# Making the high halves of the mixer's weights on GpSimd instead of ScalarE, in a two-layer encoder

## The chip, the core and the metric

The kernel runs on one core of a Trainium2 chip. The core has five engines with their own instruction queues: TensorE (PE in the profile; its weight loads are shown apart as PEld), VectorE (DVE), ScalarE (ACT), GpSimd (POOL) and SyncE (SP, which here only issues DMAs). Each queue runs in order, and an instruction waits on semaphores for what other engines or DMAs must have done. The metric is the device time of one execution in microseconds (us), less being better. Before the change it is 616.48 us, the median of three runs (616.14 to 616.51).

## What is computed

Two encoder layers over 256 tokens of width 1024. Each layer has a mixer and a feed-forward part, all in float32:

```python
def mixer_sublayer(x, ...):
    h = rms_norm(x, n1)
    proj = h @ w_in_l                       # 1024 -> 2560
    qa, ka, va, qd, kd, vd, qc, kc, vc = jnp.split(proj, cuts, axis=-1)
    ...                                     # q and k: rms_norm per head, rotary for d and c
    out_a = neighbourhood_attention(...)    # 4 heads
    out_d = dilated_window_attention(...)   # 6 heads
    out_c = gqa_block_attention(...)        # 6 query heads, 2 key/value heads
    mix = jnp.concatenate([rms_norm(out_a, ...), rms_norm(out_d, ...), rms_norm(out_c, ...)], axis=-1)
    return x + mix @ w_out_l                # 1024 -> 1024

def channel_sublayer(x, n2, w_gu, cw, cb, w_dn):
    h = rms_norm(x, n2)
    g, u = jnp.split(h @ w_gu, 2, axis=-1)  # 1024 -> 2 x 2816
    g = depthwise_conv_centred(g, cw, cb)
    return x + (jax.nn.gelu(g, approximate=False) * u) @ w_dn
```

## The kernel before, in words

**Split products.** TensorE multiplies fp32r numbers, so each float32 operand is written as a high part (the number copied into the type fp32r) and a low part (the number less its high part, again fp32r). A product then takes three matmuls: high by high, high by low, low by high (`mm3`, line 636). The weights arrive as float32 and are split on the core.

**Weight units.** All weights are cut into units of at most 2048 numbers per partition, in the order in which TensorE needs them (`units_of`, line 544). A layer has 18 units for its mixer and 33 for its feed-forward. The mixer's are, by the names in `PROJ_NAMES`: two each for dq, dk, dv, cq (8 units, 1536 wide), one for ckv, two for aqk, one for av (4 units, 2048 wide), and six for the output projection (four 1536 and two 1024 wide). `PER_LAYER` is 51 and `LAST_OUT` is 18, so `i % PER_LAYER < LAST_OUT` holds for unit `i` if it belongs to a mixer.

**What happens to a unit.** `load(i)` (line 581) has SP fetch it into one of four buffers `raw`. `split(i)` (line 607) makes the high part in one of two buffers `hi` and the low part in one of two buffers `lo`, in chunks: 384 wide for the 1536-wide projection units, 512 wide for most others, and 1024 for the feed-forward's down units. For each chunk ScalarE copies `raw` into `hi`, and VectorE subtracts: `lo = raw - hi`. Both inputs of that subtraction lie in SBUF. A `hi` buffer comes free when TensorE has finished the unit two before, a `raw` buffer when VectorE has made the last low chunk from it; then SP can fetch the unit four later. The six output-projection units of the second layer are an exception: `keep` (line 565) splits them during the first layer's feed-forward, puts both parts into DRAM, and GpSimd's DMA queue fetches them back, so `split` has nothing to do for them.

**Other work in the mixer.** The queries and keys are normalised per head (`normed`, line 901): ScalarE squares, VectorE or ScalarE sums, GpSimd computes `rstd` by two small instructions (a scale-and-add called `ms`, and a power called `rstd`), and VectorE or ScalarE scales. `rotated` (line 931) is five or more VectorE instructions on SBUF operands (`sw`, `z`). GpSimd also builds the rotary tables (`cd`, `sd`, `cc`, `sc`), spreads the neighbourhood bias with one copy of 28 partitions by 1984 (`na_repeat`, line 756), adds squares (`sqm`) and computes the group `rstd` that the output projections wait for (`group_rstd`, line 1073). Softmax and the transposed probabilities go over ScalarE and VectorE.

**Order.** The program does not emit instructions directly. `Plan` records every operation with its dependencies; `order()` (line 303) then goes through them with a table of costs (`cost`, line 416) and of hand-over times between engines, and always emits the operation that its own clock says can start first, the earlier in the program on a tie. So every instruction is issued from one line (413), and a changed cost or engine for one operation may change the order of all others, on all engines.

Of the kernel before, what the change touches and what calls it, by code (L numbers as in the profile page):

```python
# [37 lines left out]
BANK = 512  # L38
# [183 lines left out]
class Plan:  # L222
# [30 lines left out]
    def add(self, engine, method, args, kw):  # L253
# [14 lines left out]
        if method == "matmul" and not kw["start"]:  # L268
            ins.append(args[0])
        o.ns, o.size = cost(engine.name, method, args, kw, ins)  # L270
        o.before, o.after, o.first, o.tiles = set(), [], [], []
        for v in ins + outs:
# [143 lines left out]
def cost(engine, method, args, kw, ins):  # L416

    out = args[0]
    if method == "dma_start":
        w = out if isinstance(out, View) else args[1]  # L420
        small = min(out.shape[-1], args[1].shape[-1]) < 128
        return 460, 4 * math.prod(w.shape) * (2 if small else 1)
    n = out.width()
    psum = any(v.tile.pool.psum for v in ins)
    if engine == "PE":
        if method == "transpose":
            return 110, 0
        n = args[2].width()
        if args[1].dtype == F32:
            return 108, 0  # L430
        if args[1].shape[0] < P:
            return n / 4.8 + 15, 0
        return n / (2.4 if args[1].dtype == F32R else 1.2) + 2.5, 0
    if engine == "ACT":
        extra = 93 * sum(isinstance(kw.get(k), View) for k in ("scale", "bias")) + 90 * ("accum_out" in kw)
        return 0.833 * n + (47 if psum else 94) + extra, 0
    if engine == "DVE":
        if method in ("reduce_sum", "reduce_max"):
            n = args[1].width()
        per = 1.04  # L440
        if method in ("tensor_copy", "tensor_scalar_mul") and not psum:
            per = 0.52
        if method == "tensor_tensor_reduce":
            per = 1.3
        return per * n + (130 if method == "scalar_tensor_tensor" or method == "tensor_scalar_mul" and n > 16 else 70), 0
    if method == "memset":
        return 40 + 0.9 * n, 0
    if method == "tensor_copy":
        return 3.4 * n, 0
    if kw.get("op") == ALU.pow:  # L450
        return 300 + 165 * n, 0
    return 2.2 * n + 160, 0
# [3 lines left out]
def encoder_kernel(  # L456
# [21 lines left out]
    nc = Plan(tc)  # L478
# [82 lines left out]
    PER_LAYER = len(views) // DEPTH  # L561
    LAST_OUT = PER_LAYER - len(FFN)
# [44 lines left out]
    def split(i):  # L607
        v = views[i]
        a, b = v.shape[1], v.shape[2]
        n = a * b  # L610
        raw = raws[i]
        hi = wp.tile([P, UNIT], F32R, tag="hi", name=f"hi{i}", bufs=PARTS)
        lo = wp.tile([P, UNIT], F32R, tag="lo", name=f"lo{i}", bufs=PARTS)
        h = b if i < 2 else b * max(1, CHUNK // b)
        if i in kept:
            for d, z in zip(kept[i], (hi, lo)):
                nc.gpsimd.dma_start(z[:, :n], d)
        for c in range(0, n if i not in kept else 0, h):
            e = min(c + h, n)
            nc.scalar.copy(hi[:, c:e], raw[:, c:e])  # L620
            nc.vector.tensor_tensor(lo[:, c:e], raw[:, c:e], hi[:, c:e].bitcast(F32), op=ALU.subtract)
        r = lambda z: z[:, :n].rearrange("p (a b) -> p a b", b=b)
        parts.append((r(hi), r(lo)))

    def unit():

        i = taken[0]
        taken[0] += 1
        with nc.later(SPLIT_LATER):
            while len(raws) < min(i + AHEAD + RAWS - PARTS, len(views)):  # L630
                load(len(raws))
            while len(parts) < min(i + AHEAD, len(views)):
                split(len(parts))
        return parts[i]
# [181 lines left out]
    for l in range(DEPTH):  # L816
# [3 lines left out]
        if l == 0:  # L820
            gains_T(0, 1)
            split(0)
# [624 lines left out]
```

## Time and profile before

| | us |
|---|---|
| median of three runs | 616.48 |
| the profiled execution, whole | 616.62 |
| its span in the trace | 614.9 |
| PE busy | 605.8 |
| DVE busy | 487.4 |
| ACT busy | 428.1 |
| POOL busy | 82.5 |

The whole time of the profiled execution is 1.7 us more than its span. The granted TensorE clock was 0.999. Times inside the trace are given in us from the start of the span. The first layer's mixer takes about the first 128 us, its feed-forward runs to about 312, the second layer's mixer to about 426, the second feed-forward to the end. Busy times are unions per engine; a matmul's end is modelled, so PE's busy share says that PE was never long without an instruction, not that it ran at its peak. In the chain of waits, a stretch that is "PE" from piece to piece is one in which TensorE was held up by nothing but itself.

### The profile page before, as it was taken

How to read it: one execution, taken by the hardware profiler on the slowest of the kernel's cores; microseconds unless marked ns; L12 is line 12 of the kernel's file. 1: busy time of each engine (PE TensorE's matmuls, PEld its weight loads, DVE VectorE, ACT ScalarE, POOL GpSimd, SP SyncE). 2: the span in 40 equal slices, each digit the busy share in tenths (PEclk: the TensorE clock that was granted, in tenths of full speed). 3: DMA queues.
4: the chain of work that ended last, by engine and by line, in shares of the span. 5: the costliest groups of instructions: out<-in, count | busy, mean ns of one | idle time of the engine just before them, and what ended most of it. 6: DMA issues, size and time to landing. Idle time of an engine off the chain costs nothing.

```text
span 614.9 us, 9864 instructions
## 1 busy us (share of the span) xinstructions
PE 605.8 (99%) x3484; PEld 523.8 (85%) x3484; DVE 487.4 (79%) x1000; ACT 428.1 (70%) x1064; POOL 82.5 (13%) x136
## 2 busy tenths in 40 slices
PE   8999999999999999999999999999999999999997
PEld 6998878888888888888899988887888888888885
DVE  4898989897777988887867797867977777777774
ACT  6788989686566676666588898866755656556651
POOL 2731230211400000000022212332000000000000
PEclk9999999999999999999999999999999999999999
DMA  8794312655596999978444744553565556555501
GB/s 279 273 290 156 102 36 86 227 191 194 169 244 237 366 350 325 312 272 277 154 151 153 243 136 173 201 179 119 200 228 174 173 202 203 173 176 202 187 20 68
DMA packets 85073, 121.44 MB, mean 198 GB/s; under 512 B 9864, under 2 KB 69608, under 8 KB 85024
## 3 DMA queue, kind: packets, MB, share of 16 engines
q1 hardware_dynamic: 82752, 112.17, 55.3%
q0 software_dynamic: 1728, 8.39, 3.8%
q8 instruction: 27, 0.44, 0.3%
q10 hardware_dynamic: 544, 0.26, 0.2%
q14 instruction: 22, 0.18, 0.1%
HBM read 110.93 MB, written 9.88 MB: 196 GB/s over the span
## 4 chain that ended last, share of the span: by engine, by line
PE 93%; DVE 2%; ACT 2%; issue 1%; DMA 1%; POOL 0%; SPq 0%; DVEq 0%; ACTq 0%
PE psw_w L413 50%; PE psa_a L413 43%; DVE const_x L413 1%; ACT act_s2k L413 1%; DMA wp_raw<-in_w_in_dram 1%; DVE act_hT L413 1%; ACT act_hT L413 1%; ACT wp_hi L413 0%; DVE wp_lo L413 0%; POOL small_rstd L413 0%; ACT act_mixT_hi L413 0%; POOL small_ms L413 0%; SPq L413 0%; DVE act_mixT_lo L413 0%; DVE small_ss L413 0%
## 5 line engine op out<-in xcount | busy, mean ns | idle before, releaser
L413 DVE TENSOR_TENSOR wp_lo<-wp_raw,wp_hi 128x512 fp32r<-128x512 f32 (+2 forms) x332 | 232.9, 732 | 43.8 <-ACT wp_hi L413 42.3
L413 PE MATMUL psw_w<-act_hT,wp_hi 128*128 128x512 f32 x704 | 248.6, 397 | 0.4 <-DVE act_hT L413 0.4
L413 ACT CAST wp_hi<-wp_raw 128x512 fp32r<-128x512 f32 (+2 forms) x332 | 203.2, 661 | 27.0 <-PE psw_w L413 15.5
L413 PE MATMUL psw_w<-act_hT,wp_lo 128*128 128x256 f32 x704 | 196.5, 280 | 0.0
L413 PEld LDWEIGHTS psw_w<-act_hT,wp_hi 128*128 128x128 f32 x704 | 132.0, 188 | 32.6 <-DVE act_hT L413 1.1
L413 PEld LDWEIGHTS psw_w<-act_hT,wp_lo 128*128 128x128 f32 x704 | 132.7, 189 | 1.1
L413 PE MATMUL psa_a<-wp_hi,act_hT 128*128 128x384 f32 (+2 forms) x448 | 112.8, 332 | 0.7 <-ACT act_hT L413 0.5
L413 ACT COPY act_s2k<-psw_w 128x256 f32<-128x256 f32 x88 | 32.3, 372 | 74.5 <-PE psw_w L413 74.5
L413 PEld LDWEIGHTS psa_a<-wp_hi,act_hT 128*128 128x128 f32 x448 | 77.9, 189 | 3.8 <-ACT act_hT L413 1.0
L413 PE MATMUL psa_a<-wp_lo,act_hT 128*128 128x384 f32 (+2 forms) x224 | 74.8, 335 | 0.0
L413 PE MATMUL psa_a<-wp_lo,act_ch 128*128 128x512 f32 x176 | 69.5, 395 | 0.0
L413 PE MATMUL psa_a<-wp_hi,act_ch 128*128 128x512 f32 x176 | 69.4, 394 | 0.0
L413 PE MATMUL psa_a<-wp_hi,act_cl 128*128 128x512 f32 x176 | 65.8, 394 | 0.0
L413 DVE TENSOR_TENSOR act_s2k<-psw_w,act_s2k 128x256 f32<-128x256 f32 x88 | 36.8, 422 | 30.1 <-ACT act_s2k L413 29.7
L413 PEld LDWEIGHTS psa_a<-wp_lo,act_hT 128*128 128x128 f32 x224 | 42.3, 189 | 2.3 <-DVE wp_lo L413 1.3
L413 PEld LDWEIGHTS psa_a<-wp_hi,act_cl 128*128 128x128 f32 x176 | 33.2, 188 | 7.8
L413 PEld LDWEIGHTS psa_a<-wp_hi,act_ch 128*128 128x128 f32 x176 | 33.1, 188 | 7.8
L413 PEld LDWEIGHTS psa_a<-wp_lo,act_ch 128*128 128x128 f32 x176 | 33.1, 188 | 6.9
L413 DVE SCALAR_TENSOR_TENSOR act_s2k<-act_s2k,act_cw,act_s2k 128x255 f32<-128x255 f32 x88 | 36.9, 478 | 1.5 <-ACT act_s2k L413 1.3
L413 POOL TENSOR_TENSOR small_rstd<-small_ms,const_mh 128x6 f32<-128x6 f32 (+2 forms) x26 | 31.4, 1208 | 2.2
L413 ACT ACTIVATE act_s2k<-act_s2k,act_cw 128x256 f32<-128x256 f32 x44 | 24.1, 595 | 10.0 <-DVE act_s2k L413 9.6
L413 PE MATMUL psw_w<-act_ch,const_v 128*128 128x256 f32 x128 | 28.6, 286 | 1.1 <-ACT act_s2k L413 1.1
(112 smaller groups left out, 779.1 us busy)
## 6 DMA issues: line engine op xcount, KB each, us to landing
wp_raw<-in_w_gate_up_dram SPq DMA_DIRECT2D x44, 1024.0 KB, 5.1
wp_raw<-in_w_down_dram SPq DMA_DIRECT2D x22, 1024.0 KB, 4.8
wp_raw<-in_w_in_dram SPq DMA_DIRECT2D x14, 768.0 KB, 5.5
wp_raw<-in_w_in_dram SPq DMA_DIRECT2D x8, 1024.0 KB, 5.6
wp_raw<-in_w_out_dram SPq DMA_DIRECT2D x8, 768.0 KB, 6.3
dram_khi<-act_mixT_hi SPq DMA_DIRECT2D x4, 768.0 KB, 4.4
dram_klo<-act_mixT_lo SPq DMA_DIRECT2D x4, 768.0 KB, 5.8
wp_lo<-dram_klo POOLq DMA_DIRECT2D x4, 768.0 KB, 4.8
```

The source lines that it names most:

```text
L413: getattr(o.engine.real, o.method)(*map(real, o.args), **{k: real(v) for k, v in o.kw.items()})
```

## The change

In `split`, the high part of each chunk of a mixer unit is made by `gpsimd.tensor_copy` in place of `scalar.copy`, from the third unit of the program on. The first two units, all feed-forward units, and the units that `keep` handles stay with ScalarE. The planner's cost of a GpSimd copy of up to 512 elements becomes 0.92 n + 150 ns; wider ones (the bias copy) keep 3.4 n.

```diff
@@ cost
     if method == "tensor_copy":
-        return 3.4 * n, 0
+        return (3.4 * n if n > BANK else 0.92 * n + 150), 0
@@ split
         for c in range(0, n if i not in kept else 0, h):
             e = min(c + h, n)
-            nc.scalar.copy(hi[:, c:e], raw[:, c:e])
+            if i >= 2 and i % PER_LAYER < LAST_OUT:
+                nc.gpsimd.tensor_copy(hi[:, c:e], raw[:, c:e])
+            else:
+                nc.scalar.copy(hi[:, c:e], raw[:, c:e])
             nc.vector.tensor_tensor(lo[:, c:e], raw[:, c:e], hi[:, c:e].bitcast(F32), op=ALU.subtract)
```

In the emitted program 56 copies of 128x384 and 48 of 128x512 move from ScalarE's queue to GpSimd's; the number of instructions of every other kind stays the same, and their order changes.

## The prediction

> **What bounds the kernel now.** I read the engine totals first, then the busy time by stage, then the chain of waits.
>
> ```profile
> span 614.9 us, 9864 instructions
> PE 605.8 (99%) x3484; PEld 523.8 (85%) x3484; DVE 487.4 (79%) x1000; ACT 428.1 (70%) x1064; POOL 82.5 (13%) x136
> ```
>
> TensorE is without an instruction for only 9.1 us of the span. So work taken from ScalarE is worth little by itself; worth something are only the places where TensorE waits. The busy time by stage (columns: stretch and length, then PE, PEld, DVE, ACT, POOL with instruction counts, clock, DMA) gives the slack of the others:
>
> ```profile
> 14.00:60.00 46.00, 45.91 (x291) 43.32 (x292) 40.25 (x102) 38.09 (x154) 21.24 (x34) 1.00 0.83 251
> 60.00:115.00 55.00, 53.52 (x380) 46.33 (x379) 49.78 (x133) 48.89 (x139) 11.61 (x17) 1.00 0.27 88
> 312.00:372.00 60.00, 59.99 (x382) 56.06 (x380) 49.08 (x144) 52.51 (x191) 14.55 (x21) 1.00 0.50 163
> ```
>
> In the three stretches in which the mixers split weights, VectorE is idle for 5.75, 5.2 and 10.9 us: it is the next bound behind TensorE. The chain of waits has the first mixer's projections as one run of TensorE; then there is one break in each mixer before its end:
>
> ```profile
> 14.09 15.14 PE psa_a L413 x81
> 29.88 7.47 PE psa_a L413 x43
> ...
> 82.02 0.02 issue
> 82.86 1.03 ACT act_s2k L413 x4
> 85.43 0.44 PE psw_w L413 x2
> 382.31 0.02 issue
> 383.08 0.92 ACT act_s2k L413 x4
> 384.05 1.36 PE psw_w L413 x10
> ```
>
> From 82.02 to 85.43 and from 382.31 to 384.05 the chain lies on ScalarE and VectorE: 3.4 and 1.7 us, together 5.1 us. That is all a quicker ScalarE can win inside the mixers. The profiled execution took 616.62 us, 1.7 us over its span and 0.14 us above the median of 616.48; I make the sum against 616.6.
>
> **What leaves ScalarE.** 56 copies of 384 and 48 of 512.
>
> ```profile
> L413 ACT CAST wp_hi<-wp_raw 128x512 fp32r<-128x512 f32 x224 | 127.0, 621 | 3.9 <-PE psa_a L413 3.3 <-PE psw_w L413 0.4
> L413 ACT CAST wp_hi<-wp_raw 128x384 fp32r<-128x384 f32 x64 | 29.9, 536 | 6.3 <-DMA wp_raw<-in_w_in_dram 3.8 <-DVE wp_lo L413 1.7 <-PE psa_a L413 0.6
> ```
>
> 56 x 0.536 + 48 x 0.621 = 59.8 us of ScalarE, all beside TensorE's run but for part of the two breaks, which are mostly ScalarE's softmax. ScalarE's queue there gets shorter, yet the softmax still waits for its own inputs, so I take half: 2.6 us won, with 0 and 5.1 as ends.
>
> **What GpSimd takes on.** No row shows GpSimd copying to fp32r at this width. The nearest are:
>
> ```profile
> L413 POOL COPY act_nab<-act_few 28x1984 f32<-28x1984 f32 x2 | 3.7, 1834 | 22.9 <-DMA act_few<-in_rpb_dram 22.9
> L413 POOL TENSOR_TENSOR act_sqm<-act_sqm,act_sqm 128x256 f32<-128x256 f32 x10 | 7.3, 734 | 32.0 <-ACT act_sqm L413 32.0
> L413 POOL TENSOR_TENSOR act_cdk<-const_rot,const_gk 128x128 f32<-128x128 f32 x2 | 0.9, 454 | 0.0
> ```
>
> The copy has 0.92 ns per element. The two-input rows give (734 - 454)/128 = 2.19 ns per element and a fixed part of 454 - 280 = 174 ns. One input at the copy's rate without a fixed part makes 0.355 us for 384 and 0.473 us for 512; at the two-input rate it is 1.01 and 1.29 us. The operation has one input, so I take the copy's rate plus the fixed part: 0.53 and 0.64 us, in all 56 x 0.53 + 48 x 0.64 = 60.4 us, about what ScalarE needed. From 14 to 60 that is 24 x 0.53 + 12 x 0.64 = 20.4 us on top of 21.24: 41.6 of 46 us, so GpSimd fits, but only just. [...]
>
> **What that does to VectorE.** Here the trace speaks against the change. First the VectorE operations beside the bias copy, and that copy, then a VectorE subtraction and two small GpSimd products; last the spreads of both kinds of small operation:
>
> ```profile
> 24.50 2.01 DVE L413 TENSOR_TENSOR act_sw<-act_z,act_sdq 128x48 f32<-128x48 f32 x2
> 24.61 1.83 POOL L413 COPY act_nab<-act_few 28x1984 f32<-28x1984 f32 x1
> 153.08 1.28 DVE L413 TENSOR_TENSOR wp_lo<-wp_raw,wp_hi 128x1024 fp32r<-128x1024 f32 x1 [1.56 <-ACT wp_hi L413]
> 153.06 1.38 POOL L413 TENSOR_TENSOR act_sdq<-const_rot,const_gq 128x16 f32<-128x16 f32 x2
> L413 DVE TENSOR_TENSOR act_sw<-act_z,act_sdq x8: 202/209/1864, 21.4 to 325.5; 128x48 f32<-128x48 f32 x8
> L413 POOL TENSOR_TENSOR act_sdq<-const_rot,const_gq x4: 212/219/1200, 21.1 to 153.2; 128x16 f32<-128x16 f32 x4
> ```
>
> A VectorE product with both inputs in SBUF, 0.21 us as a rule, took 1.864 us beside GpSimd's copy and ended with it. The other way round, a GpSimd product of 0.22 us took up to 1.2 us beside VectorE's subtraction, which has both inputs in SBUF as well. So the two exclude each other while GpSimd reads. The wait was 1.86 - 0.20 = 1.66 of the copy's 1.83 us: I let a new copy hold VectorE for its elements alone, 0.355 or 0.473 us. How often it meets such an operation I take from the share of the stage that they fill (subtractions first, then the rotary's `sw` part):
>
> ```profile
> 14.00:60.00 46.00, 19.72 (x36) 1.00 0.83 251
> 312.00:372.00 60.00, 23.82 (x43) 1.00 0.50 163
> 14.00:60.00 46.00, 7.09 (x22) 1.00 0.83 251
> 312.00:372.00 60.00, 6.55 (x32) 1.00 0.50 163
> 60.00:115.00 55.00, 14.44 (x22) 1.00 0.27 88
> ```
>
> The shares are 26.8/46 = 0.58, 30.4/60 = 0.51 and, from 60 to 115 (subtractions only), 14.4/55 = 0.26.
> - 14 to 60: units 2 to 10, 24 copies of 384 and 12 of 512, hold 8.5 + 5.7 = 14.2 us; x 0.58 = 8.3 us. VectorE's idle 5.75 us is partly dependence, in a fixed order; I let half absorb it: 5.4 us late, and so is TensorE, which has no gaps to catch up in.
> - 60 to 115: 20 copies of 512 hold 9.5 us; x 0.26 = 2.5 us, covered by half of 5.2 us: 0.
> - 312 to 372: 27 of 384 and 16 of 512 hold 17.2 us; x 0.51 = 8.7 less 5.5 = 3.2 us. Five more lie in the feed-forward before, under its cover: 0.
>
> Sum: 5.4 + 3.2 - 2.6 = 6.0 us, 616.6 + 6.0 = 622.6, say **623 us**. With all of VectorE's idle time usable and both breaks gone it is 8.3 - 5.75 - 5.1 = -2.6, 614 us; with none usable and no break gone 8.3 + 2.5 + 8.7 = +19.5, 636 us.
>
> **What is moved on the queues.** GpSimd's queue is in order, so a copy that waits for a free high buffer stands before the `ms` and `rstd` behind it.
>
> ```profile
> POOL small_ms L413 <- ACT act_s2k L413: 12.9, 3, 9.6
> DVE act_z L413 <- POOL small_rstd L413: 2.0, 2, 1.2
> ```
>
> From 14 to 60 VectorE waited 2.0 us for `rstd`; four copies in front of one add up to 4 x 0.53 = 2.1 us each time. TensorE has the next projections to run meanwhile, so 0; if they run out it is 2.1 us for each of the first two `rstd`. On SP, the load of unit 9 now stands behind the two bias reads, which in turn need GpSimd's bias copy:
>
> ```profile
> 32.13 0.39 SPq L413 DMA_DIRECT2D wp_raw<-in_w_in_dram  x1
> 34.85 1.96 SPq L413 DMA_DIRECT2D act_nab<-dram_scr  x2
> 44.81 0.65 ACT L413 CAST wp_hi<-wp_raw 128x512 fp32r<-128x512 f32 x1
> ```
>
> It moves from 32.1 to about 36.8 and is first used at 44.8; 8 us cover a transfer: 0, and if the bias copy is late by more than some 2 us, that excess. The planner's costs also reorder TensorE's attention work; the sum of its matmuls is unchanged, and I cost it at nothing, with the breaks as the bound (+/- 5.1 us).
>
> **Rivals.** (a) *Faster:* the copies meet VectorE in its waits and PSUM-fed operations, nothing is held, and both breaks go: 616.6 - 5.1 = 611.5 us. For it: ScalarE's relief is real. Against it: between 14 and 60 VectorE is busy 40.25 of 46 us and two thirds of that is of the excluding kind. It decides once VectorE is held less than about 2.9 us in 14 to 60 and 5.5 us in 312 to 372. (b) *Slower by more:* a copy holds VectorE for its whole 0.53 or 0.64 us: 20.4 x 0.58 + 12.8 x 0.26 + 24.5 x 0.51 = 27.6 us, less the half slacks of 2.9, 2.6 and 5.5, no break won: +16.6, 633 us. For it: GpSimd would be full from 14 to 60. Against it stands a row of its own:
>
> ```profile
> 27.59 1.52 POOL L413 TENSOR_TENSOR small_rstd<-small_ms,const_mh 128x6 f32<-128x6 f32 x1
> 27.84 0.25 DVE L413 TENSOR_TENSOR act_z<-act_z,act_sw 128x96 f32<-128x96 f32 x1
> ```
>
> A two-input GpSimd power of 1.52 us did not hold the VectorE sum inside it (0.25 us, 27.84 to 28.09): it is the reading that excludes, not the instruction. The Trainium skill's "SBUF — State Buffer", section "Who interferes with whom", has the pair of ports locked for the whole instruction; by that this rival's 633 us would come out, and the trace bears that rule out only in part. (c) *No change:* what is held and what is won cancel, 616.5 us.
>
> **How the numbers follow.** Forecast 0.53 (618 to 633), (b) 0.20, (a) 0.18, (c) 0.09. Slower by over 0.2% (1.2 us, about what a measurement of this kernel can tell from none) is 0.73, the same 0.09, faster 0.18. The range goes from (a) at 611 to 642, short of (b) without slack (+27.6, 644): below it lies half of (a), above it a part of (b).
>
> **What would show it.** Right: `wp_lo` and `sw` longer than 0.55 and 0.21 us beside GpSimd copies, up to about 1 us; more VectorE waits for `wp_hi`; TensorE waiting for `wp_lo` between 14 and 60; the feed-forward starting at about 133 instead of 128, lasting as long as before. Wrong: `wp_lo` at its old mean and the first mixer no longer, or copies over 0.8 us, or `rstd` as the releaser of the long waits.

## The result, and the profile after

The changed kernel takes 631.08 us (median, 630.81 to 631.32), the kernel before on the same chip 616.31 us (615.87 to 616.51). The ratio is 1.0244 with a 95% interval of 1.0231 to 1.0256: slower by 14.8 us. The forecast was 623.0, slower by 6.0. The direction is right, the size is not.

First the head of the page after: span, busy time by engine, and the shares of the chain of waits.

```profile
span 629.0 us, 9933 instructions
...
PE 610.1 (97%) x3484; PEld 523.4 (83%) x3484; DVE 507.2 (81%) x1000; ACT 381.8 (61%) x960; POOL 156.7 (25%) x240
...
PE 82%; DVE 7%; POOL 5%; ACT 3%; issue 2%; POOLq 0%; ACTq 0%; DVEq 0%
```

The shares of the chain were, before:

```profile
PE 93%; DVE 2%; ACT 2%; issue 1%; DMA 1%; POOL 0%; SPq 0%; DVEq 0%; ACTq 0%
```

TensorE was without an instruction for 9.1 us of the span before, and is now for 18.9; in the chain GpSimd has gone from 0 to 5% and VectorE from 2 to 7%. VectorE executes the same 1000 instructions, but is busy 19.8 us longer (487.4 before). GpSimd is busy 74.2 us longer, though the copies themselves take 68.0 us of it. Next, one group before and three after (mean ns of one behind the busy time, then the idle time before it and what ended that):

```profile
L413 DVE TENSOR_TENSOR wp_lo<-wp_raw,wp_hi 128x384 fp32r<-128x384 f32 x64 | 33.1, 556 | 7.1 <-ACT wp_hi L413 7.1
```

```profile
L413 POOL CAST wp_hi<-wp_raw 128x512 fp32r<-128x512 f32 x48 | 34.4, 749 | 6.8 <-PE psa_a L413 6.7
L413 POOL CAST wp_hi<-wp_raw 128x384 fp32r<-128x384 f32 x56 | 33.6, 639 | 147.3 <-PE psa_a L413 147.2
...
L413 DVE TENSOR_TENSOR wp_lo<-wp_raw,wp_hi 128x384 fp32r<-128x384 f32 x64 | 41.6, 687 | 5.3 <-ACT wp_hi L413 2.7 <-POOL wp_hi L413 2.6
```

The subtractions of 384 columns have gone from 556 to 687 ns. The copies take 639 and 749 ns on average. Where nothing stands against them they are shorter; the spreads of tiles (shortest, median, longest in ns) show it, and after them one lone copy from the timeline:

```profile
L413 POOL CAST wp_hi<-wp_raw x104: 496/628/1140, 15.5 to 381.6; 128x384 fp32r<-128x384 f32 x56, 128x512 fp32r<-128x512 f32 x48
L413 DVE TENSOR_TENSOR wp_lo<-wp_raw,wp_hi x332: 541/685/2189, 6.4 to 614.9; 128x512 fp32r<-128x512 f32 x112, 128x384 fp32r<-128x384 f32 x32, 128x1024 fp32r<-128x1024 f32 x22
L413 DVE TENSOR_TENSOR act_sw<-act_z,act_scq x16: 246/432/659, 56.9 to 368.2; 128x96 f32<-128x96 f32 x16
```

```profile
110.27 0.61 POOL L413 CAST wp_hi<-wp_raw 128x512 fp32r<-128x512 f32 x1 [0.19 <-PE psa_a L413]
```

Alone, a copy takes 0.50 us (384) and 0.61 us (512); the longest took 1.14. The hold goes both ways: beside the copies a subtraction of 384 columns took some 0.85 us, an `sw` product of 96 columns up to 0.66 where its median was 0.25 before. The longest subtraction, 2.19 us, is not the work of a moved copy: it lies from 29.80 to 31.99, beside the bias copy (29.42 to 31.57), which held an `sw` product before.

The busy time by stage (columns as in the prediction) is given for the same three places; the stretches are longer because the mixers are:

```profile
14.00:68.00 54.00, 46.45 (x279) 41.13 (x280) 47.99 (x95) 21.20 (x112) 47.99 (x70) 1.00 0.68 199
68.00:124.00 56.00, 56.00 (x394) 48.57 (x393) 52.78 (x140) 42.46 (x128) 24.94 (x37) 1.00 0.28 95
318.40:380.00 61.60, 56.98 (x364) 52.43 (x363) 52.15 (x122) 30.59 (x141) 40.05 (x59) 1.00 0.43 144
```

In the first row TensorE, 45.91 of 46 us before, now has an instruction in 46.45 of 54: 7.6 us are lost here. VectorE and GpSimd are each busy 47.99 of the 54 us, ScalarE only 21.20. The chain of waits shows what the loss consists of:

```profile
15.55 2.70 POOL wp_hi L413 x4
...
18.34 0.84 POOL small_ms L413
...
19.27 1.36 POOL small_rstd L413
...
26.98 2.48 POOL wp_hi L413 x4
29.46 2.11 POOL act_nab L413
...
31.67 0.85 POOL small_ms L413
...
32.59 1.53 POOL small_rstd L413
...
34.15 1.35 ACT act_z L413 x6
...
40.52 4.34 PE psa_a L413 x22
```

Where the chain before had one run of TensorE from 14.09 on, it now lies mostly on GpSimd from 15.55 to 34.12: four copies, and only behind them the `ms` and `rstd` that the keys wait for, then more copies and the bias copy, then the next `rstd`. TensorE is back on it at 40.52. The feed-forward begins where TensorE runs these 82 matmuls, in the chain before and after:

```profile
127.69 14.59 PE psw_w L413 x82
```

```profile
136.32 14.38 PE psw_w L413 x82
```

That is 8.6 us later. The list of waits after (us in all, times, longest) names three hand-overs. The first and the third are the same hand-over as TensorE's weight loads and its matmuls see it, so they are not to be added. The first was 1.3 us in the kernel before, the second 4.2, and the third does not appear in its list:

```profile
PEld psa_a L413 <- DVE wp_lo L413: 10.4, 14, 1.5
...
DVE act_z L413 <- POOL small_rstd L413: 6.7, 9, 1.5
...
PE psa_a L413 <- DVE wp_lo L413: 6.2, 11, 1.1
```

The feed-forward's regular steps then stay late by 8.2 to 8.4 us, so they are unchanged. The second one begins 14.2 us late; the second mixer has added 6.0.

### The profile page after: what moved, and what is told of

Read it like the earlier page. It is cut to its first block, busy times and chain, and to the rows that moved or that the text cites. A ratio compares the mean times of both kernels' runs of the same rounds, so it can differ in the third digit from the quotient of the medians.

```text
span 629.0 us, 9933 instructions
## 1 busy us (share of the span) xinstructions
PE 610.1 (97%) x3484; PEld 523.4 (83%) x3484; DVE 507.2 (81%) x1000; ACT 381.8 (61%) x960; POOL 156.7 (25%) x240
## 4 chain that ended last, share of the span: by engine, by line
PE 82%; DVE 7%; POOL 5%; ACT 3%; issue 2%; POOLq 0%; ACTq 0%; DVEq 0%
PE psw_w L413 49%; PE psa_a L413 33%; DVE act_z L413 2%; POOL wp_hi L413 2%; DVE wp_lo L413 2%; DVE act_sw L413 1%; POOL small_rstd L413 1%; ACT act_s2k L413 1%; ACT act_hT L413 1%; DVE const_x L413 1%; POOL small_ms L413 1%; ACT wp_hi L413 1%; DVE act_hT L413 0%; ACT act_z L413 0%; POOL act_nab L413 0%
## 5 line engine op out<-in xcount | busy, mean ns | idle before, releaser
L413 DVE TENSOR_TENSOR wp_lo<-wp_raw,wp_hi 128x512 fp32r<-128x512 f32 (+2 forms) x332 | 244.6, 768 | 39.4 <-ACT wp_hi L413 35.5
L413 ACT CAST wp_hi<-wp_raw 128x512 fp32r<-128x512 f32 (+2 forms) x228 | 149.4, 698 | 24.5 <-PE psw_w L413 15.4
L413 POOL CAST wp_hi<-wp_raw 128x384 fp32r<-128x384 f32 (+1 forms) x104 | 68.1, 690 | 154.1 <-PE psa_a L413 153.9
L413 ACT ACTIVATE act_s2k<-psa_a 128x64 f32<-128x64 f32 (+2 forms) x80 | 17.9, 253 | 29.8 <-PE psa_a L413 29.8
```

What stands on the lines that cost most here:

```text
L413: getattr(o.engine.real, o.method)(*map(real, o.args), **{k: real(v) for k, v in o.kw.items()})
```

## The experiments

The edits are to the kernel before or to the changed one, as said. "Order" is the order in which the planner emitted the instructions. All losses are against the kernel before, on the same chip.

### Is it the engine or the order?

The first keeps the changed kernel's plan and order, but has ScalarE execute the copies. The second keeps the order of before and has GpSimd execute them.

```diff
@@ emit, in the changed kernel (order on ScalarE)
+                if o.engine.name == "POOL" and o.method == "tensor_copy" and o.args[0].dtype == F32R:
+                    self.scalar.real.copy(*map(real, o.args))
+                    continue
@@ emit and split, in the kernel before (old order on GpSimd)
+                if o.kw.get("on") == "gpsimd":
+                    self.gpsimd.real.tensor_copy(*map(real, o.args))
+                    continue
...
+            if i >= 2 and i % PER_LAYER < LAST_OUT:
+                nc.scalar.copy(hi[:, c:e], raw[:, c:e], on="gpsimd")
```

> Planned exactly as the changed kernel, so TensorE, VectorE, GpSimd and SyncE keep its order, but the 104 copies are executed on ScalarE at the places that the plan gave them on GpSimd. Theory H (copies on GpSimd and VectorE's operations with two SBUF inputs hold each other up): the hold is gone, 616 to 620 us, VectorE busy back at about 487 us. Theory Q (GpSimd's queue is full, and ms and rstd stand behind copies): also gone, 616 to 620 us. Theory O (the planner's new order is itself the loss): 626 to 632 us.

> Planned exactly as the kernel before, so every other engine keeps the old order, but the 104 copies are executed on GpSimd where the plan had them on ScalarE. H: the hold is there, 628 to 640 us, and VectorE's subtractions of 384 average about 0.69 us. Q: slower as well, 628 to 640 us. O: 615 to 619 us, since the order is the old one.

The new order on ScalarE took 628.6 us (ratio 1.0212, 1.0196 to 1.0227), the old order on GpSimd 634.66 us (1.031, 1.0294 to 1.0325). So GpSimd's copies cost 19 us in the order of before: the new order does not make the loss, it saves some 4 us of it. The first run missed what theories H and Q expected of it, and taken by itself it says that the order alone is bad. The next pair tells why it can't be read so.

### The order with hardly any copying

Here each moved copy treats only its first 8 columns. The dependence from `raw` over `hi` to `lo` stays, the time of the copy nearly goes. Two fills at the start, for columns that would else never be written, are not shown.

```diff
@@ emit, in the changed kernel (and, for the second run, in the old order)
+                if o.engine.name == "POOL" and o.method == "tensor_copy" and o.args[0].dtype == F32R:
+                    self.gpsimd.real.tensor_copy(*[real(v[:, 0:8]) for v in o.args])
+                    continue
```

> The changed kernel with its order on every engine, but each of the 104 GpSimd copies takes only the first 8 columns of its chunk; the rest of the high part is left as it was, so the products are not those of the reference. What remains is the new order with almost no reading by GpSimd. Theory H (hold): the loss goes, 614 to 619 us, VectorE busy at about 487 us. Theory O (the new order is a loss by itself, as the run with this order on ScalarE allows): 624 to 630 us.

> The same cut, products again not those of the reference, in the order of the kernel before. H and O both say that nothing is left that costs: 612 to 618 us; what it is below the kernel before bounds what ScalarE's relief can win. If it stays above 620 us, the small copies in GpSimd's queue delay ms and rstd (theory Q).

They took 616.81 us (1.003, 1.0017 to 1.0044) and 616.85 us (1.0019, 1.0009 to 1.0028). Of the one in the new order, the page's busy times and then the copies among the groups:

```profile
PE 605.7 (99%) x3484; PEld 523.1 (85%) x3484; DVE 487.1 (79%) x1000; ACT 381.8 (62%) x960; POOL 112.5 (18%) x242
```

```profile
L419 POOL CAST wp_hi<-wp_raw 128x8 fp32r<-128x8 f32 x104 | 26.9, 292 | 165.9 <-PE psa_a L421 164.9 <-DVE small_nm L421 0.4 <-DVE const_v L421 0.3
```

ScalarE is relieved by the full 46 us, VectorE is no busier than before (487.1), GpSimd's copies cost 0.29 us each on average, and the time is that of before or a little more. Two things follow. The new order by itself is worth nothing and costs about 1.2 us (2.7 at the upper end of the interval); so what `order_on_act` lost came from 60 us of copies put into ScalarE's queue at places planned for GpSimd (argued, not measured apart). And relief of ScalarE wins nothing that shows, in either order; a gain as small as what the small copies themselves cost on GpSimd could hide behind them.

### What the copies do to others: ghost work

In the order of before, with ScalarE making the high parts as ever, GpSimd gets an extra instruction per chunk whose output nobody reads: a copy from the same `raw`, or a fill, which reads nothing.

```diff
@@ emit, in the kernel before; one of the three GpSimd lines in each run; the second scratch line in long_fills alone
+                if o.kw.get("on") == "both":
+                    n = o.args[0].width()
+                    scratch = self.spare.tile([P, BANK], F32R, tag="spare", name=f"spare{i}", bufs=4)
+                    scratch = self.spare.tile([P, 744], F32R, tag="spare", name=f"spare{i}", bufs=3)   # long_fills
+                    self.scalar.real.copy(*map(real, o.args))
+                    self.gpsimd.real.tensor_copy(scratch[:, :n], real(o.args[1]))         # ghost_copy
+                    self.gpsimd.real.memset(scratch[:, :n].bitcast(F32), 0.0)             # ghost_memset
+                    self.gpsimd.real.memset(scratch[:, : {384: 672, 512: 744}[n]].bitcast(F32), 0.0)  # long_fills
+                    continue
```

> The kernel before with its order, ScalarE still makes every high part; behind each of the 104 mixer copies GpSimd copies the same chunk once more into a spare buffer that nobody reads. H: the hold alone, +6 to +15 us (622 to 631 us), VectorE busy up by 12 to 20 us. Q: ms and rstd stand behind the extra copies, also +4 to +12 us. O: no change, 616 to 618 us.

> As the run with extra copies, but GpSimd fills the spare buffer with zeros instead of copying: about the same time on GpSimd's queue (0.4 to 0.6 us each), without reading SBUF. H: VectorE is not held, VectorE busy stays at 487 to 490 us and the time at 616 to 619 us. Q: the queue is as full as with the copies, so the loss is the same as in that run, +4 us or more. O: 616 to 618 us.

> The kernel before with its order; behind each of the 104 mixer copies GpSimd fills 672 or 744 columns of a spare buffer with zeros, about 0.68 and 0.73 us each, as long as the extra copies took there, without reading SBUF. If ms and rstd behind a fuller GpSimd queue make a large part of the loss: 621 us or more. If VectorE's hold makes it: 617 to 619.5 us, and VectorE busy stays at 487 to 489 us.

The ghost copies took 630.36 us (1.0241, 1.0224 to 1.0259), which is the changed kernel's loss without ScalarE's relief and without any dependence on GpSimd's result. The fills of equal width took 617.76 us (1.0033, 1.002 to 1.0046), the long ones 624.15 us (1.0141, 1.0124 to 1.0158). For each, the page's busy times and then rows of its groups by shape. The ghost copies:

```profile
PE 610.4 (97%) x3484; PEld 522.9 (83%) x3484; DVE 507.2 (81%) x1000; ACT 428.7 (68%) x1064; POOL 153.7 (24%) x240
```

```profile
L419 DVE TENSOR_TENSOR wp_lo<-wp_raw,wp_hi 128x384 fp32r<-128x384 f32 x64 | 43.3, 716 | 3.1 <-ACT wp_hi L419 1.7 <-ACT wp_hi L416 1.3
```

The equal fills:

```profile
PE 606.1 (98%) x3484; PEld 523.4 (85%) x3484; DVE 487.5 (79%) x1000; ACT 428.7 (70%) x1064; POOL 127.7 (21%) x240
```

```profile
L417 POOL MEMSET spare<- 128x384 f32 x56 | 21.2, 416 | 0.2
L419 DVE TENSOR_TENSOR wp_lo<-wp_raw,wp_hi 128x384 fp32r<-128x384 f32 x64 | 32.9, 553 | 6.5 <-ACT wp_hi L416 3.6 <-ACT wp_hi L419 2.8
```

The long fills:

```profile
PE 608.9 (98%) x3484; PEld 524.8 (84%) x3484; DVE 487.7 (78%) x1000; ACT 428.7 (69%) x1064; POOL 149.3 (24%) x240
```

```profile
L417 POOL MEMSET spare<- 128x672 f32 x56 | 34.7, 661 | 0.1
L417 POOL MEMSET spare<- 128x744 f32 x48 | 32.9, 725 | 0.1
```

Copies hold VectorE (507.2, subtractions 716 ns); fills, however long, don't (487.5 and 487.7). The subtractions of 384 columns average 553 ns beside the equal fills and 581 beside the long ones; there one of them met the bias copy, as in the changed kernel. But the long fills, which fill GpSimd about as long as the changed kernel's copies (0.66 and 0.73 against 0.64 and 0.75 us), cost 8.9 us without holding anybody.

Part of that is not paid by the change. In the stage table of the long fills the clock (the column behind the instruction counts of POOL) is below 1.00:

```profile
14.00:68.00 54.00, 51.27 (x306) 46.91 (x307) 43.29 (x108) 40.96 (x163) 43.17 (x71) 0.97 0.73 215
```

The granted clock was 0.50 from 41.0 to 44.2, after TensorE had had an instruction for only 1.5 of the 3 us from 38 to 41, and 0.996 on average in all four runs; the changed kernel had 0.999 to 1.0. At half the clock those 3.2 us cost at most 1.6, so by estimate some 7 us of the 8.9 are left for the queue's waits. The wait behind this is in the lists of waits (us in all, times, longest), first of the kernel before, then of the one with long fills:

```profile
DVE act_z L413 <- POOL small_rstd L413: 4.2, 5, 1.2
...
ACT act_z L413 <- POOL small_rstd L413: 0.7, 1, 0.7
```

```profile
DVE act_z L419 <- POOL small_rstd L419: 7.8, 8, 1.6
ACT act_z L419 <- POOL small_rstd L419: 5.2, 2, 4.0
```

VectorE's row alone would not tell: the 8-column kernel, which lost 1.2 us, has 6.8 there. The wait of 4.0 us on ScalarE does. ScalarE stood still from 31.9 to 35.9 for `rstd`, with the next high halves behind it in its own queue, and TensorE then waited for `wp_hi` and `wp_lo`.

GpSimd's timeline of the kernel with long fills (start, length, engine, operation):

```profile
27.64 2.20 POOL L419 COPY act_nab<-act_few 28x1984 f32<-28x1984 f32 x1
29.79 3.66 POOL L417 MEMSET spare<- 128x672 f32 x6
33.56 0.28 POOL L419 TENSOR_SCALAR small_ms<-small_ss,small_he 128x6 f32<-128x6 f32 x1
33.89 0.66 POOL L417 MEMSET spare<- 128x672 f32 x1
34.52 1.33 POOL L419 TENSOR_TENSOR small_rstd<-small_ms,const_mh 128x6 f32<-128x6 f32 x1
```

Six fills stand before one `ms` of 0.28 us, and a seventh between it and its `rstd`: the queue is in order, so the small work that others wait for is late. With the equal fills, 0.42 and 0.53 us per chunk, GpSimd is busy for 36.09 of the 46 us from 14 to 60 and the loss is 2.1 us; with the long ones it is busy for 42.96.

### The hold alone, and both without the exclusion

To give VectorE the added time alone, it subtracts the first 40 columns of each of the 104 chunks once more; GpSimd gets nothing. Then the same together with the long fills.

```diff
@@ emit, in the kernel before (redo_cols), and in long_fills (redo_and_fills)
+                if o.kw.get("on") == "again":
+                    self.vector.real.tensor_tensor(*map(real, o.args), op=o.kw["op"])
+                    self.vector.real.tensor_tensor(*[real(v[:, 0:40]) for v in o.args], op=o.kw["op"])
+                    continue
@@ split
+            again = dict(on="again") if i >= 2 and i % PER_LAYER < LAST_OUT else {}
-            nc.vector.tensor_tensor(lo[:, c:e], raw[:, c:e], hi[:, c:e].bitcast(F32), op=ALU.subtract)
+            nc.vector.tensor_tensor(lo[:, c:e], raw[:, c:e], hi[:, c:e].bitcast(F32), op=ALU.subtract, **again)
```

> Before's order, ScalarE makes the high halves, GpSimd gets nothing new. Behind each of the 104 subtractions in the mixers VectorE subtracts the first 40 columns once more (about 0.19 us each), so VectorE is busy about 20 us longer, as in the changed kernel, while GpSimd's queue stays as it was. If VectorE's added time by itself makes most of the loss (theory V): 625 to 630 us. If the loss needs a full GpSimd queue (theory Q): at most the 6 us of the prediction's sum, 617 to 622 us.

> The same, and beside it on GpSimd a fill of 672 or 744 columns per chunk (0.66 or 0.73 us, nothing read from SBUF), as long as the changed kernel's copies. Both parts of the changed kernel's load without the exclusion itself. If the two explain its loss (V and Q together): 629 to 633 us, as the changed kernel. If the exclusion does more than add time to the two engines: below 627 us. If the fills' 8.9 us and the redone columns' time hide behind each other: about 624 us.

The repeated columns alone took 623.12 us (1.0123, 1.0097 to 1.0149), both together 627.72 us (1.0194, 1.0167 to 1.0222). The page's busy times of the first, the repeated columns among its groups, and the busy times of the joint kernel:

```profile
PE 607.7 (98%) x3484; PEld 522.6 (84%) x3484; DVE 507.4 (82%) x1104; ACT 429.2 (69%) x1064; POOL 86.0 (14%) x136
```

```profile
L415 DVE TENSOR_TENSOR wp_lo<-wp_raw,wp_hi 128x40 fp32r<-128x40 f32 x104 | 22.7, 218 | 3.6
```

```profile
PE 610.5 (97%) x3484; PEld 522.1 (83%) x3484; DVE 507.4 (81%) x1104; ACT 429.4 (69%) x1064; POOL 150.0 (24%) x240
```

VectorE's 20.0 us more (the changed kernel has 19.8) cost 7.5 us where GpSimd's queue is as before: some 12.5 us are absorbed. The measurement lies just above the bound of the one expectation (622) and below the other's (625): VectorE makes about half of the loss. Its four runs differ in the granted clock: two at 0.999 and 1.0 took 621.78 and 622.38 us, two at 0.997 some 2 us more, so at the full clock the loss is nearer 6.5. The joint run gives 12.1 us, outside all three of its expected ranges: less than 7.5 + 8.9 = 16.4, partly because its trace has no such stretch at half the clock (0.999 on average), and otherwise, as is argued and not measured, because some of the two waits lie beside each other; and less than the 14.8 of the change (whose interval, from 1.0231 up, lies above this one's). Where the feed-forward starts in the chain tells in which mixer the rest lies (columns alone, both, then the long fills alone, one kernel each):

```profile
132.42 14.38 PE psw_w L417 x82
```

```profile
136.05 14.59 PE psw_w L423 x82
```

```profile
133.85 14.59 PE psw_w L419 x82
```

Against 127.69 the three are late by 4.7, 8.4 and 6.2 us, the changed kernel by 8.6. So in the first mixer the two parts together make up the loss, without the exclusion itself. The 2.7 us that are missing in the whole lie behind it: the second feed-forward is late by 11.3 us in the joint kernel and by 14.2 in the changed one.

### How the loss grows with the copied part

In the changed kernel's order, half and three quarters of each chunk's columns are copied (the edit of the 8-column run with `v.width() // 2` and `v.width() * 3 // 4`).

```diff
@@ emit, in the changed kernel
+                    self.gpsimd.real.tensor_copy(*[real(v[:, 0 : v.width() // 2]) for v in o.args])
```

> The changed kernel with its order, each GpSimd copy taking the first half of its chunk; the products are not those of the reference. The hold by the prediction's rule halves, from 19.5 to about 9.8 us. If VectorE's idle time absorbs the first part of a hold (the prediction let 11 us of it do so): 617 to 619 us. If the loss is in proportion to the hold, between 616.8 us with 8 columns and 631 us with whole chunks: 622 to 626 us.

> The changed kernel with its order, each copy taking three quarters of its chunk; the products are not those of the reference. VectorE is held some 13 to 15 us. If the idle time absorbs about 7 us and the rest reaches the end in full, as 8.1 us held for 3.0 lost (half) and 19.8 for 14.3 (whole) allow: 623 to 626 us. A straight line from the half to the whole gives 625.5 us.

Half took 619.79 us (1.0058, 1.0043 to 1.0073), three quarters 625.28 us (1.0156, 1.0139 to 1.0173). The half lies between its two expected ranges, the three quarters within theirs. With the 8-column run and the change itself as the ends, each loss against its own run of before:

| columns copied | us lost | VectorE busy | GpSimd busy |
|---|---|---|---|
| 8 | 1.2 | 487.1 | 112.5 |
| half | 3.6 | 495.2 | 135.5 |
| three quarters | 9.5 | 500.2 | 147.4 |
| all | 14.8 | 507.2 | 156.7 |

The loss is not proportional: the first 8.1 us of hold cost 2.4 us, the next 12.0 cost 11.2. Hold and fullness of the queue grow together here, so this table by itself can't say which of them makes the bend.

### By place, fewer of them, and the planner told

The copies moved in the first mixer only, in the second only, in the first layer's output projection only, and for every second chunk of a unit (50 copies). Last, a planner that is told the copies' lengthened times (639 and 749 ns).

```diff
@@ split, in the changed kernel: one condition in each run
-            if i >= 2 and i % PER_LAYER < LAST_OUT:
+            if 2 <= i < LAST_OUT:                                # layer1_only
+            if PER_LAYER <= i < PER_LAYER + LAST_OUT:            # layer2_only
+            if LAST_OUT - len(OUT_ORDER) <= i < LAST_OUT:        # out_only
+            if i >= 2 and i % PER_LAYER < LAST_OUT and c // h % 2:   # every_other
@@ cost, in the changed kernel (plan_held)
-        return (3.4 * n if n > BANK else 0.92 * n + 150), 0
+        return (3.4 * n if n > BANK else 0.86 * n + 309), 0
```

> Only the first layer's 16 units (56 copies) go to GpSimd. H with the places as read from the trace of the changed kernel (8.2 us in the first mixer, 6.0 in the second): +8.2 us, 623 to 626 us. If the two layers do not add up: below 620 or above 628 us.

> Only the second layer's 12 projection units (48 copies) go to GpSimd. H: the 6.0 us that the second mixer lost in the trace of the changed kernel, 620 to 623 us; with the 9.5 us of the run with the first layer alone the two then add up to about the whole loss.

> Only the first layer's six output-projection units (16 copies of 512) go to GpSimd, between about 60 and 115 us, where the subtractions fill 0.26 of the stage. H: hold 16 x 0.47 x 0.26 = 2.0 us, covered by VectorE's idle 5 us, and at most the break of 3.4 us is won: 613 to 617 us. O: a new order again costs something, 618 us or more.

> Every second chunk of the same units goes to GpSimd, the others stay on ScalarE, 52 copies in all. If the hold absorbs into idle time while ScalarE is still relieved of 30 us: 614 to 618 us. In proportion to the hold: 622 to 626 us.

> The changed kernel with the planner told what the copies took there (0.639 us for 384 and 0.749 for 512 in place of 0.50 and 0.62). If the loss is a plan made with too short copies: under 624 us. If it is the mutual hold, which no cost of a single operation describes: 628 to 633 us.

| run | copies | us | ratio, interval | VectorE busy |
|---|---|---|---|---|
| layer1_only | 56 | 625.09 | 1.0153, 1.0138 to 1.0168 | 498.2 |
| layer2_only | 48 | 621.77 | 1.0089, 1.0072 to 1.0106 | 496.7 |
| out_only | 16 | 615.18 | 0.9994, 0.9985 to 1.0003 | 488.4 |
| every_other | 50 | 620.11 | 1.0065, 1.005 to 1.008 | 493.1 |
| plan_held | 104 | 634.62 | 1.0295, 1.028 to 1.0311 | 505.3 |

The losses of the two mixers, 9.5 and 5.6 us, add up to the whole (15.1 against 14.8); VectorE's growth (10.8 and 9.3) does too. Every second chunk costs 4.0 us, between its two expected ranges. Only the output projection's copies can move at no cost (from 60 to 115, where they lie, GpSimd was busy 11.61 of 55 us), and that wins nothing that can be measured. A planner with the truer lengths does not help: the kernel takes 3.5 us more than the change. Its granted clock was lower, though (0.989 to 0.992; 13.6 us of its trace are at 0.50, worth up to 6.8 us). Without that, by estimate, it stays near 628 us, so a wrong length in the plan makes at most some 3 us of the loss.

## Why the prediction was right and wrong

**Direction and place: right.** The forecast put the loss in the two mixers, with the feed-forward starting at about 133 and lasting as long as before; it starts at 136.3, and its steps are unchanged. The new order, costed at nothing, cost about 1.2 us in the 8-column run. TensorE waits for `wp_lo` in the first mixer, subtractions and `sw` grew, and rivals (a) and (c) are out.

**The copies' price: right.** 0.53 and 0.64 us were forecast; alone they take 0.50 and 0.61. The Trainium skill's "GPSIMD Engine Reference", section 3.1, gives about 1.8 cycles per element as the best case of a tight unrolled loop, with 769 ns measured for 512 elements. This copy of 512 is quicker, 0.61 us alone, and the measurement decides. But 0.53 was taken for GpSimd's load too, and there the mean counts: 0.64 and 0.75 us, since GpSimd is held by VectorE as VectorE is by it.

**The hold of VectorE: right.** 8.3 + 2.5 + 8.7 = 19.5 us were forecast, VectorE's busy time grew by 19.8, and the single-mixer runs split it as forecast (10.8 and 9.3 against 10.8 and 8.7). That the two come within 0.3 us is closer than shares of a stage can promise. The rule that reading excludes, not the instruction, was borne out by copies against fills. Rival (b) came near in its time (633) by another road: it needed 27.6 us of hold, and 19.8 were seen. The Trainium skill's "SBUF — State Buffer", section "Who interferes with whom", has the pair of ports locked for the whole instruction, which was that rival's rule; the 19.8 us do not bear it out.

**Half of VectorE's idle time absorbs: about right.** The forecast left 5.4 + 0 + 3.2 = 8.6 us; the same added time with GpSimd's queue as before cost 7.5 (6.5 at the full clock). In the trace of its quickest run 4.7 us of that lie in the first mixer and 0.8 in the second, where 3.2 were forecast.

**The breaks (2.6 us won): wrong.** 46 us less of ScalarE won nothing that shows, in either order. Without this term the sum would have been 625.2. The relief itself was reckoned at 59.8 us and was 46.3 (428.1 to 381.8). The sum took the mean length of a copy, but the groups' busy times (29.9 us for 64 copies, 127.0 for 224) are less than count times mean, so neighbours overlap; by them it would have been 53.4.

**"TensorE has the next projections to run meanwhile, so 0": wrong, and the main miss.** This is the step on GpSimd's queue: `ms` and `rstd` behind copies were seen, priced at 2.1 us for each of two `rstd`, and set to nothing. A queue nearly as full as the change makes it (149.3 us busy against 156.7) costs 8.9 us with VectorE not held at all (some 7 without the stretch at half the clock), and 4.6 us where VectorE has its added time as well (12.1 less 7.5). The load was reckoned at 41.6 of 46 us, which "fits, but only just"; but a queue that is busy 47.99 of 54 us and runs in order delays the small instructions in it, and through `rstd` the keys and queries, and with them the other engines' queues and TensorE. In the trace after, the `rstd` behind the bias copy starts at 32.59, after the copies, where it started at 27.59 before. Of the signs that the prediction gave for being wrong, one came half true: `rstd` stands in the chain of waits three times up to 56.1, but the longest wait for it in the list is 1.5 us, against 1.2 before. No group of copies averaged over 0.8 us. The sign that VectorE would wait more for `wp_hi` failed; the groups show less of it (5.3 us of idle time before the 384 subtractions, 7.1 before).

**The sum with what was measured.** In place of 8.6 (VectorE) + 0 (queue) - 2.6 (breaks) = 6.0 us the runs give 7.5 + 4.6 (the queue on top of VectorE) + 0, and 2.7 that is not accounted for: 14.8. The intervals leave each of the three parts some 1.7 us either way. Of the 8.8 us missed, the queue is the largest part.

**What stays open.** The two loads without the exclusion make 12.1 of the 14.8 us. In the first mixer they make all of it; the 2.7 us left lie in the second. The new order is not needed for them: the ghost copies, in the order of before, lose 14.7 us as well, and in their trace the second feed-forward is 13.25 us late, against 11.3 with the two loads. What the ghost copies have and the two loads lack is the exclusion itself. That it costs more there because it falls unevenly was not tried.

## What to carry to other kernels

Before moving work to an engine that looks idle, list what small work stands in its in-order queue and who waits for it, stage by stage: that small work is late before the sum of busy times fills the stage (here with GpSimd busy for 43 of 46 us, hardly with 36). Ask also what the engine shares with the one that is next to bound: a copy that reads SBUF on GpSimd holds VectorE's two-input operations and is held by them, so both get longer (here 556 to 687 ns and 0.50 to 0.64 us). Ghost work, whose output nobody reads, prices each of the two by itself, in the old order and without the gain that hides it.

## What the hardware showed that was not expected

- A GpSimd fill of 384 or 512 columns takes 0.42 or 0.53 us and leaves VectorE's subtraction at 553 ns; a GpSimd copy of the same width puts it at 716.
- A GpSimd copy of 8 columns takes 0.19 us alone (the median of 104; the mean is 0.29, as single ones lasted up to 1.30), one of 384 takes 0.50.
- 46 us less of ScalarE's busy time moved the end by nothing that shows, and 68 us of fills on GpSimd, an engine at 13%, moved it by 8.9: the share of busy time on the page told neither.
